# A one-core transformer layer: first columns of the modulation in another order with first features between them, and two groups of DVE work bound to a later point

## The chip, the cores and the metric

The kernel runs on one core of a Trainium2 chip. The metric is the device time of one execution in microseconds (us): median 2355.22 us of 3 runs, 2352.29 to 2355.99. The engines run their own instruction streams side by side: PE (TensorE, matrix products and transposes), DVE (VectorE), ACT (ScalarE), POOL (GpSimd), and SP (SyncE), which here issues most of the DMA transfers. Each engine takes its instructions in a fixed order; semaphores make it wait for what others produce.

## The reference, cut to what matters

One layer over 2048 latent tokens of width 1024, with 256 context tokens:

```
mod  = silu(c) @ w_ada + b_ada          # sh1 sc1 g1 sh2 sc2 g2, 1024 each
cmod = silu(c_ctx) @ w_ada + b_ada
hc = LN(ctx) * (1 + csc1) + csh1        # context: keys and values only
h  = LN(x) * (1 + sc1) + sh1
q, k, v, u, vg, ga, gb = split(h @ w_in)
y_attn = windowed attention (8 q heads, 2 kv heads, rope, sink, context keys)
y_gm   = gelu(u) * (ws @ LN(gelu(vg)) + bs)      # in chunks of 128 tokens
mix = (sigmoid(ga) * (y_attn @ w_pa) + sigmoid(gb) * (y_gm @ w_pb)) @ w_o
x  = LN(alpha * x + g1 * mix)
h2 = LN(x) * (1 + sc2) + sh2
x  = LN(alpha * x + g2 * moe(h2))       # 4 groups x 8 experts, top 2, SwiGLU
```

## The kernel before

Products are taken at 32 bits through two parts: every operand is split into a high part (a cast on ACT) and a low part (a subtraction on DVE, or on POOL in one place), and each product is three passes, high by high, low by high, high by low. `split` (L85) does this everywhere; `Wh` and `Wl` are the two parts of a piece of weights of 128x1024, loaded into one of three `raw` buffers by SP.

The work stands in four stages, whose limits in the trace are near 110, 560, 1470 and 2300 us.

**Start (`pass1`, before its loop over tokens).** `w_ada`'s columns for sh1 and sc1 come in four blocks of 512: blocks 0 and 1 are the shift, 2 and 3 the scale. Each block is four loads of 512 KB and 8 products (`ada_piece`, L265, 16 passes on PE). `ada_columns` (L270 to L275) copies a finished block on ACT, turns it into columns on PE, and DVE writes it into `modc`. Then come steps from the string `START`: `c0` to `c3` and `h0` to `h3` are `modulate` for the context tokens and for latent tokens 0 to 255, each for two of the eight 128-wide chunks of the width: PE transposes (L350), ACT applies scale and shift (L358, tile `hf`), the high part is taken on DVE (L364, `hTh`), the low part on DVE for the context and on POOL for latent tokens (L365, `hTl`), and for latent tokens SP writes `hf` to DRAM (`hT_d`, L367). Chunks 0 to 3 (`c0`, `c1`, `h0`, `h1`) need blocks 0 and 2; the others need 1 and 3. `x0`, `x1` and `a0`, `a1` are the k and v products for the two tiles of context and of latent tokens (L383, 24 products of 128x256 a tile); the second of the turns L394 that follow `a1` closes this stretch. `w4` to `w17` split weights. Instructions under `keep_in_program_order` keep their written order on their engine; the others are ordered by the scheduler's own simulation.

**Second pass (`pass2`)** goes over the latent tokens in four groups `g` of 512. For each, `spatial` multiplies the gated half by `wst` in eight parts (`gg`), each closed by a `scalar_tensor_tensor` on DVE (L840, in pairs), then `mixers` turns the result on PE (L850), splits it into `gh` and `gl`, and there are 8 steps `f` of gates and merge, with pieces `wf`. `between(g, f)` is called between these steps. In group 0 it appends `rows_ada` for f = 0 to 5: the other six blocks of `w_ada` for one row, as four 512 KB loads into `raw` and 8 multiply-adds on DVE (L760, L762). In groups 1 to 3 it calls `norms` for the four token tiles of the group before, for f = 0 to 3: the residual (L912), two layer norms (L94 to L100, L784, L785) and two writes. With `tc.issue_after(X)`, an instruction that is on X's engine is kept behind X; an instruction on another engine isn't bound by it. In the kernel before, `norms` is bound to `st["mixed"]`, the last split of the attention output, which is a DVE instruction.

**Experts (`moe`).** `prepare(s, j)` loads and splits pieces of the second expert's weights. `k.at[3]` is a PE instruction; the instructions of `prepare` run on ACT, DVE and SP.

The pieces that the change and the steps of the prediction touch are listed here.

Of the kernel before, what the change touches and what calls it, by code (L numbers as in the profile page):

```python
# [7 lines left out]
F32 = mybir.dt.float32  # L8
# [5 lines left out]
OP = mybir.AluOpType  # L14
# [4 lines left out]
P = 128  # L19
D = 1024  # L20
# [5 lines left out]
NQ = 8  # L26
# [107 lines left out]
            fn()  # L134


START = 'c0 c1 w5 c2 w6 w4 c3 x0 w7 h0 h1 h2 k w9 x1 h3 w8 a0 n0 a1 w10 t0 w11 t1 q0 q1 q2 q3 n1 q4 g0 q5 g1 l0 l1 w12 w14 w15 t2 l2 g2 s0 l3 g3 w17 l4 w16 s1 w13 l5'
PRM = dict(f0=0.2, f1=0.4, b1=0.4, b2=0.0, f2=0.8, f3=1.0, b3=1.2, pq=3, pk=5, mi=1, np=1, ps=16, pa=6)


# [8 lines left out]
def pass1(k):  # L149

    nc, tc, T = k.nc, k.tc, k.T
    with ExitStack() as ctx:
# [31 lines left out]
        def load_tile(t):  # L184
            load_x(t, T["x"][t * P:(t + 1) * P, :])
# [12 lines left out]
        def load_ada(i):  # L198
            if i < 16:
                ada[i] = wk.tile([P, 2, 512], F32, name="x", tag="x", bufs=4)  # L200
                pinned(nc.sync.dma_start(ada[i], T["ada1"][:, i // 4, 2 * (i % 4):2 * (i % 4) + 2, :]))

        for i in range(4):
            load_ada(i)
        cx = wk.tile([P, 2, D], F32, name="hTl", tag="hTl", bufs=2)
        for i in range(2):
            xin["c", i] = [cx[:, i, :]]
            pinned(nc.sync.dma_start(cx[:, i, :], T["ctx"][i * P:(i + 1) * P, :]))

        cols = ([(slice(2 * i, 2 * i + 2), slice(512, 768)) for i in range(4)]  # L210
                + [(slice(i, i + 1), slice(0, 512)) for i in range(8)]
# [23 lines left out]
        def norm_stats(key):  # L235
            x = xin[key]
            stats[key] = ln_stats(k, wk, x if len(x) == 2 else x[0], D, pin=key in range(2, PRM["ps"]))
# [16 lines left out]
            return x[h][:, kc * P:(kc + 1) * P]  # L254


        accs = {}

        def ada_piece(i):
            cb, kk = divmod(i, 4)  # L260
            if kk == 0:
                accs[cb] = ps.tile([2, 512], F32, name="pj", tag="pj", bufs=2)
            for j in range(2):
                kc = 2 * kk + j
                nc.tensor.matmul(accs[cb], k.sil[:, kc, :], ada[i][:, j, :], start=kc == 0, stop=kc == KC - 1)  # L265
            load_ada(i + 4)

        def ada_columns(cb):
            m2 = wk.tile([2, 512], F32, name="qr", tag="qr", bufs=1)
            nc.scalar.copy(m2, accs[cb])  # L270
            tp = ps.tile([P, 4, 2], F32, name="tr", tag="tr", bufs=1)
            for j in range(4):
                nc.tensor.transpose(tp[:, j, :], m2[:, j * P:(j + 1) * P], k.ident[0:2, 0:2])
            for s in range(2):
                nc.vector.scalar_tensor_tensor(k.modc[:, 2 * s + cb // 2, 4 * (cb % 2):4 * (cb % 2) + 4], tp[:, :, s],  # L275
                                               float(cb // 2), bcol[:, 4 * cb:4 * cb + 4], op0=OP.add, op1=OP.add)

        for i in range(16):
            ada_piece(i)
            if i in (2, 3):  # L280
                norm_stats(("c", i - 2))
            if i in (4, 5):
                norm_apply(("c", i - 4))
            if i in (4, 5):
                t = i - 4
                xin[t] = [wk.tile([P, 512], F32, name="x0", tag=("ph", "pl")[t], bufs=2) for _ in range(2)]
                for h in range(2):
                    pinned(nc.sync.dma_start(xin[t][h], T["x"][t * P:(t + 1) * P, h * 512:(h + 1) * 512]))
            if i in (8, 9):
                norm_stats(i - 8)  # L290
                norm_apply(i - 8)
            if 6 <= i < 10:
                load_w(i - 6)
            if 11 <= i < 15:
                wsplit(i - 11)
            if i > 4 and i % 4 == 1:
                ada_columns(i // 4 - 1)
        load_tile(2)
        load_tile(3)
        mk = wk.tile([P, 2, 2 * P], F32, name="hf", tag="hf", bufs=2)[:, 0, :]  # L300
        pinned(nc.sync.dma_start(mk, T["mask"]))
        sink = c.tile([P, NQ], F32, name="sink")
        pinned(nc.sync.dma_start(sink, bcast_row(T["sink"], NQ)))
        load_tab(0)
        load_tab(1)
        start[0] = False
# [398 lines left out]
def pass2(k):  # L705
    nc, tc, T = k.nc, k.tc, k.T
    k.late = k.ctx.enter_context(tc.tile_pool(name="late", bufs=1, reuse_waits="tile"))
    with ExitStack() as ctx:
# [120 lines left out]
        def spatial(g):  # L829

            uy, vv = st[g][1], st["vv"]
            if g == 0:
                tc.keep_in_program_order(nc.sync.dma_start(bst, T["bst"]))
            ws = wsplit(T["wst"].rearrange("p g q -> p (g q)"))
            for gg in range(8):
                tp = tr_bank()
                sp = tp[:, 0:256].rearrange("p (i d) -> p i d", d=HD)
                cs = slice(gg * HD, (gg + 1) * HD)
                mm3(sp, [x[:, gg * P:(gg + 1) * P] for x in ws], (vv[:, 0, :, cs], vv[:, 1, :, cs]), True, True)
                nc.vector.scalar_tensor_tensor(uy[:, 1, :, cs], sp, bst[:, gg:gg + 1], uy[:, 0, :, cs],  # L840
                                               op0=OP.add, op1=OP.mult)
# [318 lines left out]
        def between(g, f):  # L1160

            nonlocal g1, sh2, sc2, ln1g, ln1b, rws
            while due:
                due.pop(0)()
            if g == 0:
                if f < 6:
                    due.append(rows_ada(g1 if f < 2 else sh2 if f < 4 else sc2, f, 1.0 if f // 2 == 2 else 0.0))
                return
            t = 4 * (g - 1) + f
            if 1 <= f < 5:  # L1170
                turned[t - 1] = logit_rows(h2s[t - 1])
# [315 lines left out]
def moe(k):  # L1487
    nc, tc, T = k.nc, k.tc, k.T
    with ExitStack() as ctx:
# [213 lines left out]
        for i in range(NBL):  # L1703
            s, _, _, last = blocks[i]
            hidden(i)
            gate(i)
            with tc.issue_after(k.at[3]) if not i else nullcontext():
                rows(i + 1)
                if not i:
                    early_output(1)  # L1710
            if i:
                gather(i + GA)
                output(i - 1)
                evacuate(i - 1)
# [195 lines left out]
```

## Time and profile before

| | us |
|---|---|
| median of 3 runs | 2355.22 |
| profiled execution, own time | 2353.14 |
| its span, first to last instruction | 2351.1 |
| PE busy in the span | 2206.8 |
| DVE busy | 1749.7 |
| ACT busy | 1197.9 |
| POOL busy | 622.1 |

The profile is of one execution. It is read in this way: the busy times say which engine is nearest to the span, the table by windows says where that engine isn't busy, and the waits of an engine say what released it. A row `L383 <- POOL hTl L365: 2.6, 2, 1.5` says that the engine stood 2.6 us in all before line 383, twice, 1.5 us the longest, for what line 365 made on POOL.

### The profile page before, as it was taken

To read this page: it belongs to the slowest core of one execution; us is meant where nothing else is said; L and a number is where in the kernel's file an instruction comes from. 1 tells how busy PE (TensorE), PEld (TensorE's weight loads), DVE (VectorE), ACT (ScalarE), POOL (GpSimd) and SP (SyncE) were. 2 spreads that over 40 slices of the span, in tenths; PEclk is the share of its full clock that TensorE was granted. 3 is DMA by queue.
4 is the path that set the end of the run, shared out by engine and by line. 5 is a ranking of instruction groups with operands and counts; after the bars stand their busy time and mean duration, and the time that the engine had idled before them with its cause. 6 is when DMAs were issued, how large, how long until landed. Compare 5 with 4: busy or idle time off the path is not lost. (4 is left out here: it accounts for less than half of the span.)

```text
span 2351.1 us, 31795 instructions
## 1 busy us (share of the span) xinstructions
PE 2206.8 (94%) x11269; PEld 1813.8 (77%) x11269; DVE 1749.7 (74%) x3029; ACT 1197.9 (51%) x1673; POOL 622.1 (26%) x518
## 2 busy tenths in 40 slices
PE   7899999999999999999999999899999999999980
PEld 3789999997778788878887887587877777877760
DVE  4778888887675677577557858578898878696977
ACT  3566666655433333333424333356666666564755
POOL 1333333331000101011101113323353445243324
PEclk9899999999999999999999999899999999999995
DMA  8111111115674446544344434489998989797967
GB/s 313 64 59 59 55 59 42 41 42 170 197 239 153 152 144 185 161 151 150 112 156 153 153 117 188 152 271 322 338 339 290 330 280 331 234 360 235 337 215 295
DMA packets 126710, 449.34 MB, mean 191 GB/s; under 512 B 20763, under 2 KB 42195, under 8 KB 101973
## 3 DMA queue, kind: packets, MB, share of 16 engines
q1 hardware_dynamic: 113684, 405.29, 49.8%
q0 software_dynamic: 12864, 41.98, 7.5%
q8 instruction: 90, 1.47, 0.3%
q14 instruction: 72, 0.58, 0.1%
HBM read 382.66 MB, written 64.57 MB: 190 GB/s over the span
## 5 line engine op out<-in xcount | busy, mean ns | idle before, releaser
L85 DVE TENSOR_TENSOR mWl<-mraw,mWh 128x2048 fp32r<-128x2048 f32 x192 | 450.2, 2362 | 89.9 <-ACT mWh L85 89.0
L85 ACT CAST mWh<-mraw 128x2048 fp32r<-128x2048 f32 x192 | 363.7, 1909 | 176.0 <-PE h L1612 82.2
L100 POOL TENSOR_TENSOR mv<-mv,mhalf 128x1 f32<-128x1 f32 x58 | 56.7, 981 | 664.2 <-DVE mv L99 657.9
L1612 PE MATMUL h<-mWh,xh 128*128 128x512 f32 x784 | 218.2, 400 | 12.4 <-ACT xh L85 7.9
L85 DVE TENSOR_TENSOR Wl<-raw,Wh 128x1024 fp32r<-128x1024 f32 x140 | 170.4, 1220 | 77.5 <-ACT Wh L85 76.8
L85 ACT CAST Wh<-raw 128x1024 fp32r<-128x1024 f32 x140 | 146.1, 1047 | 139.0 <-PE mm L743 66.2
L1612 PE MATMUL h<-mWl,xh 128*128 128x512 f32 x784 | 214.7, 394 | 0.0
L742 PE MATMUL mm<-hh,Wl 128*128 128x512 f32 x512 | 201.1, 393 | 5.5 <-DVE Wl L85 5.5
L741 PE MATMUL mm<-hh,Wh 128*128 128x512 f32 x512 | 202.7, 396 | 2.3 <-ACT Wh L85 1.6
L743 PE MATMUL mm<-hl,Wh 128*128 128x512 f32 x512 | 200.8, 392 | 0.0
L1660 POOL DMA_INDIRECT acc_d<-yo,lst x48 | 144.1, 3003 | 153.6 <-DVE yo L1654 95.7
L1612 PEld LDWEIGHTS h<-mWh,xh 128*128 128x128 f32 x784 | 145.3, 189 | 46.5 <-ACT xh L85 9.8
L1612 PEld LDWEIGHTS h<-mWl,xh 128*128 128x128 f32 x784 | 146.8, 188 | 32.9
L383 PE MATMUL pj<-wq,hTh 128*128 128x256 f32 (+1 forms) x544 | 151.9, 355 | 1.6 <-DVE hTh L364 1.4
L1577 POOL DMA_INDIRECT xg<-h_d,lst x48 | 79.9, 1665 | 206.6 <-PE tr L1598 98.7
L85 ACT CAST ph<-pt 128x512 fp32r<-128x512 f32 x184 | 93.4, 520 | 73.4 <-PE pt L572 69.9
L1612 PE MATMUL h<-mWh,xl 128*128 128x512 f32 x464 | 127.0, 394 | 0.0
L548 ACT ACTIVATE Sb<-Sb,mx 128x641 f32<-128x641 f32 (+1 forms) x128 | 105.4, 824 | 40.3 <-DVE mx L543 31.3
L541 DVE CUSTOM_DVE_ANT_0 Sb<-S,mask,sink 128x640 f32<-128x640 f32 (+1 forms) x128 | 110.2, 861 | 18.9 <-PE S L537 15.8
L85 DVE TENSOR_TENSOR pl<-pt,ph 128x512 fp32r<-128x512 f32 x184 | 109.0, 604 | 19.2 <-ACT ph L85 17.4
L1612 PE MATMUL y<-mWh,gh 128*128 128x512 f32 x392 | 112.2, 406 | 8.1 <-ACT mWh L85 3.3
L742 PEld LDWEIGHTS mm<-hh,Wl 128*128 128x128 f32 x512 | 96.7, 189 | 26.4 <-DVE Wl L85 7.1
(385 smaller groups left out, 5371.9 us busy)
## 6 DMA issues: line engine op xcount, KB each, us to landing
mraw<-mw SPq DMA_DIRECT2D x192, 1024.0 KB, 7.3
raw<-wf SPq DMA_DIRECT2D x96, 512.0 KB, 3.7
raw<-ada SPq DMA_DIRECT2D x32, 512.0 KB, 4.8
raw<-wo SPq DMA_DIRECT2D x32, 512.0 KB, 4.2
x<-x SPq DMA_DIRECT2D x30, 512.0 KB, 4.3
x<-ada SPq DMA_DIRECT2D x16, 512.0 KB, 5.4
hT_d<-hf SPq DMA_DIRECT2D x32, 256.0 KB, 2.2
raw<-hT_d SPq DMA_DIRECT2D x16, 512.0 KB, 4.9
```

The lines of the kernel that those rows point to most:

```text
L85: return k.nc.scalar.copy(hi, src), (eng or k.nc.vector).tensor_sub(lo, src, hi)
L100: nc.gpsimd.tensor_tensor(mv[:, 3:4], mv[:, 2:3], k.mhalf, op=OP.pow)
L383: ins = nc.tensor.matmul(box[0][:, :n], x[:, kc, ts], wpart(y, kc, slice(c0, c0 + n))[:, 0, :], start=q == 0, stop=q == 3 * KC - 1)
L541: nc.vector.tensor_tensor_reduce(x[:, :nk], S[:, :nk], mask[:, mi, :nk], 1.0, sink[:, h:h + 1], OP.add, OP.max, mx[:, s:s + 1])
L548: nc.scalar.activation(Sb[s][:, :nk + 1], Sb[s][:, :nk + 1], AF.Exp, bias=mx[:, 2 + s:3 + s], scale=1.0, accum_out=mx[:, 4 + s:5 + s])
L741: nc.tensor.matmul(out, lh, rh, start=first, stop=False)
L742: nc.tensor.matmul(out, ll, rh, start=False, stop=False)
L743: nc.tensor.matmul(out, lh, rl, start=False, stop=last)
L1577: ins = nc.gpsimd.indirect_dma_start(out=xg[i][0:n, :], out_offset=None, in_=k.h2_d[:, :], in_offset=bass.IndirectOffsetOnAxis(ap=place(i) ...
L1612: ins = nc.tensor.matmul(accs[m], a[:, ks], b[:, c0:c0 + 512], start=first and i + j == 0, stop=last and j == 1 and i == len(t) - 1)
L1660: nc.gpsimd.indirect_dma_start(out=k.acc_d[:, :], out_offset=bass.IndirectOffsetOnAxis(ap=l[:, 0:1], axis=0), in_=yo[0:n, :], in_offset=No ...
```

## The change

There are five edits. (A) The blocks of `w_ada` are loaded and used in the order 0, 2, 1, 3; the steps c0, c1 run behind piece 10, and h0, h1 behind piece 12 of the 16, inside the loop over the pieces, and are taken out of `START`. The context tokens are loaded as four tiles of 128x512 rather than two of 128x1024. The mask goes through another buffer. The function definitions that the steps need are moved ahead of the loop unchanged, which shifts their lines: L350 becomes L322, L383 becomes L355. (B) `rows_ada` is called for f = 1 to 6 and bound to `st["sp"]`, the last L840 instruction so far. (C) `norms` for f above 0 is bound to the same. (D) In the experts, two calls of `prepare` are bound to `k.at[3]`. The fifth edit stores `st["sp"]`.

```diff
-START = 'c0 c1 w5 c2 w6 w4 c3 x0 w7 h0 h1 h2 k w9 x1 h3 w8 a0 n0 a1 ...
+START = 'w5 c2 w6 w4 c3 x0 w7 h2 k w9 x1 h3 w8 a0 n0 a1 ...
...
-                pinned(nc.sync.dma_start(ada[i], T["ada1"][:, i // 4, 2 * (i % 4):2 * (i % 4) + 2, :]))
+                pinned(nc.sync.dma_start(ada[i], T["ada1"][:, (0, 2, 1, 3)[i // 4], 2 * (i % 4):2 * (i % 4) + 2, :]))
...
-        cx = wk.tile([P, 2, D], F32, name="hTl", tag="hTl", bufs=2)
         for i in range(2):
-            xin["c", i] = [cx[:, i, :]]
-            pinned(nc.sync.dma_start(cx[:, i, :], T["ctx"][i * P:(i + 1) * P, :]))
+            xin["c", i] = [wk.tile([P, 512], F32, name="cx", tag=n, bufs=2 if i else 1) for n in (("oT", "oT") if i else ("t1", "t2"))]
+            for h in range(2):
+                pinned(nc.sync.dma_start(xin["c", i][h], T["ctx"][i * P:(i + 1) * P, h * 512:(h + 1) * 512]))
...
             if i > 4 and i % 4 == 1:
                 ada_columns(i // 4 - 1)
+            for n in {10: ("c0", "c1"), 12: ("h0", "h1")}.get(i, ()):
+                steps[n]()
...
-                nc.vector.scalar_tensor_tensor(uy[:, 1, :, cs], sp, bst[:, gg:gg + 1], uy[:, 0, :, cs],
-                                               op0=OP.add, op1=OP.mult)
+                st["sp"] = nc.vector.scalar_tensor_tensor(uy[:, 1, :, cs], sp, bst[:, gg:gg + 1], uy[:, 0, :, cs],
+                                                          op0=OP.add, op1=OP.mult).ins
...
-                if f < 6:
-                    due.append(rows_ada(g1 if f < 2 else sh2 if f < 4 else sc2, f, 1.0 if f // 2 == 2 else 0.0))
+                if 1 <= f < 7:
+                    with tc.issue_after(st["sp"]):
+                        due.append(rows_ada(g1 if f < 3 else sh2 if f < 5 else sc2, f - 1, 1.0 if f > 4 else 0.0))
...
-                with tc.issue_after(st["mixed"]):
+                with tc.issue_after(st["sp" if f else "mixed"]):
                     h2s[t] = norms(t, rr[f])
...
             if i == 1:
-                prepare(1, 0)
-                prepare(1, 1)
+                with tc.issue_after(k.at[3]):
+                    prepare(1, 0)
+                    prepare(1, 1)
```

How the instructions then stand on PE at the start, first before. L265 are the passes over blocks of `w_ada`, L273 the turns of a finished block, L350 the transposes of context tokens (`hTl` is the buffer that held them), and L383 the k and v products.

```order
L273 MATMUL tr<-ident,qr 128x2 x4
L265 MATMUL pj<-x,sil 2x512 x6
L273 MATMUL tr<-ident,qr 128x2 x4
L265 MATMUL pj<-x,sil 2x512 x6
L273 MATMUL tr<-ident,qr 128x2 x4
L265 MATMUL pj<-x,sil 2x512 x6
L350 MATMUL pt<-ident,hTl 128x128 x4
L273 MATMUL tr<-ident,qr 128x2 x4
L350 MATMUL pt<-ident,hTl 128x128 x4
L383 MATMUL pj<-wq_114,hTh 128x256
L383 MATMUL pj<-wq_114,hTl 128x256
L383 MATMUL pj<-wq_115,hTh 128x256
```

And on PE after the change, in two pieces of the same stretch: `x_192` and `x_202` are latent tokens, `cx` is the context, and the last rows shown are the last passes of the loop.

```order
L322 MATMUL pt<-ident,x_192 128x128
L322 MATMUL pt<-ident,x_202 128x128
L274 MATMUL tr<-ident,qr 128x2 x4
L322 MATMUL pt<-ident,cx 128x128 x4
L265 MATMUL pj<-x,sil 2x512 x2
L322 MATMUL pt<-ident,cx 128x128 x4
L355 MATMUL pj<-wq_114,hTh 128x256
L355 MATMUL pj<-wq_114,hTl 128x256
L355 MATMUL pj<-wq_115,hTh 128x256
```

```order
L355 MATMUL pj<-wq_116,hTh 128x256
L355 MATMUL pj<-wq_116,hTl 128x256
L355 MATMUL pj<-wq_119,hTh 128x256
L265 MATMUL pj<-x,sil 2x512 x4
L274 MATMUL tr<-ident,qr 128x2 x4
```

Eight transposes of latent tokens, eight more of the context and twelve k and v products now stand ahead of the last four passes of the loop; all of them stood behind the loop before.

On DVE in group 0 of the second pass, before: L760 and L762 are `rows_ada` (`aacc`), L840 closes the parts of `spatial`, `Wl` is the low part of a piece of weights.

```order
L760 TENSOR_SCALAR aacc<-raw,sil 128x512
L85 TENSOR_TENSOR Wl<-raw,Wh 128x1024
L762 SCALAR_TENSOR_TENSOR aacc<-raw,sil,aacc 128x512 x2
L94 BN_STATS st<-vg 128x6
L762 SCALAR_TENSOR_TENSOR aacc<-raw,sil,aacc 128x512
L98 BN_AGGR mv<-st 128x2
L840 SCALAR_TENSOR_TENSOR yh<-tr,bst,yh 128x4x64
L762 SCALAR_TENSOR_TENSOR aacc<-raw,sil,aacc 128x512
L99 TENSOR_SCALAR mv<-mv 128x1
L840 SCALAR_TENSOR_TENSOR yh<-tr,bst,yh 128x4x64
L762 SCALAR_TENSOR_TENSOR aacc<-raw,sil,aacc 128x512 x3
L85 TENSOR_TENSOR Wl<-raw,Wh 128x1024
```

The same place after the change, where L843 is the former L840 and L763, L765 are `rows_ada`:

```order
L843 SCALAR_TENSOR_TENSOR yh<-tr,bst,yh 128x4x64 x2
L85 TENSOR_TENSOR Wl<-raw,Wh 128x1024
L843 SCALAR_TENSOR_TENSOR yh<-tr,bst,yh 128x4x64 x2
L85 TENSOR_TENSOR Wl<-raw,Wh 128x1024
L843 SCALAR_TENSOR_TENSOR yh<-tr,bst,yh 128x4x64 x2
L85 TENSOR_TENSOR Wl<-raw,Wh 128x1024
L890 TENSOR_TENSOR sg<-sg,mm 128x512
L843 SCALAR_TENSOR_TENSOR yh<-tr,bst,yh 128x4x64 x2
L763 TENSOR_SCALAR aacc<-raw,sil 128x512
L765 SCALAR_TENSOR_TENSOR aacc<-raw,sil,aacc 128x512
```

All of `rows_ada` now stands behind the fourth pair of the closings.

On DVE in group 1, before, from the last `Wl` but two ahead of the first pair of L840: `rr` and `x` are rows in `norms`, of two tiles.

```order
L85 TENSOR_TENSOR Wl<-raw,Wh 128x1024
L98 BN_AGGR mv<-st 128x2 x2
L99 TENSOR_SCALAR mv<-mv 128x1
L784 SCALAR_TENSOR_TENSOR x<-rr,mv,sc_7747 128x1024
L99 TENSOR_SCALAR mv<-mv 128x1
L784 SCALAR_TENSOR_TENSOR rr<-rr,mv,ln1g 128x1024
L785 SCALAR_TENSOR_TENSOR x<-x,mv,sh_7489 128x1024
L785 SCALAR_TENSOR_TENSOR rr<-rr,mv,ln1b 128x1024
L85 TENSOR_TENSOR Wl<-raw,Wh 128x1024
L94 BN_STATS st<-rr 128x6 x2
L840 SCALAR_TENSOR_TENSOR yh<-tr,bst,yh 128x4x64 x2
```

After the change:

```order
L787 SCALAR_TENSOR_TENSOR x<-rr,mv,sc_7729 128x1024
L85 TENSOR_TENSOR Wl<-raw,Wh 128x1024
L788 SCALAR_TENSOR_TENSOR x<-x,mv,sh_7475 128x1024
L85 TENSOR_TENSOR Wl<-raw,Wh 128x1024
L843 SCALAR_TENSOR_TENSOR yh<-tr,bst,yh 128x4x64 x2
L85 TENSOR_TENSOR Wl<-raw,Wh 128x1024
L843 SCALAR_TENSOR_TENSOR yh<-tr,bst,yh 128x4x64 x2
L85 TENSOR_TENSOR Wl<-raw,Wh 128x1024
L843 SCALAR_TENSOR_TENSOR yh<-tr,bst,yh 128x4x64 x2
L85 TENSOR_TENSOR Wl<-raw,Wh 128x1024
L890 TENSOR_TENSOR sg<-sg,mm 128x512
L843 SCALAR_TENSOR_TENSOR yh<-tr,bst,yh 128x4x64 x2
```

The norms of the second tile are gone from between the weights' low parts; they follow behind the last pair. On PE and ACT the order in the experts is the same in both kernels.

## Rows read from the trace of the kernel before

**Rows 1.** The page's busy times: engine, us (share of the span), instructions.

```profile
PE 2206.8 (94%) x11269; PEld 1813.8 (77%) x11269; DVE 1749.7 (74%) x3029; ACT 1197.9 (51%) x1673; POOL 622.1 (26%) x518
```

**Rows 2.** Windows: length, busy us of PE, PEld, DVE, ACT, POOL, clock, DMA, GB/s.

```profile
0.00:110.00 110.00, 88.84 (x416) 55.30 (x417) 61.59 (x147) 49.83 (x93) 30.19 (x43) 0.94 0.57 198
```

**Rows 3.** Groups of PE's instructions, 0 to 40 us: busy, mean | idle before.

```profile
L265 PE MATMUL pj<-x,sil 128*2 128x512 f32 x64 | 30.5, 622 | 7.4 <-DMA x<-ada 7.3
```

**Rows 4.** Windows within the start, columns as in group 2.

```profile
20.00:40.00 20.00, 19.41 (x58) 4.38 (x57) 7.87 (x22) 7.37 (x12) 1.09 (x2) 1.00 1.01 376
...
60.00:64.00 4.00, 4.00 (x20) 4.00 (x20) 2.24 (x7) 0.27 (x1) 1.28 (x2) 0.50 0.00 0
```

**Rows 5.** PE's waits, 40 to 66 us: total us, times, longest.

```profile
PE pj L383 <- POOL hTl L365: 2.6, 2, 1.5
PE pj L383 <- DVE hTh L364: 1.4, 1, 1.4
PE pj L383 <- DVE hTl L365: 0.8, 1, 0.8
PE pt L350 <- ACT hf L358: 0.8, 2, 0.5
```

**Rows 6.** PE's timeline, 39 to 66 us: start, us, instruction [idle before].

```profile
38.47 1.45 PE L265 MATMUL pj<-x,sil 128*2 128x512 f32 x3
39.85 0.66 PE L350 MATMUL pt<-ident,hTl 128*128 128x128 f32 x4
...
45.48 0.38 PE L383 MATMUL pj<-wq,hTl 128*128 128x256 f32 x1 [0.76 <-DVE hTl L365]
...
47.51 0.28 PE L383 MATMUL pj<-wq,hTl 128*128 128x256 f32 x1
...
47.86 0.28 PE L383 MATMUL pj<-wq,hTl 128*128 128x256 f32 x1
...
65.32 0.38 PE L394 MATMUL tr<-ident,kd 128*128 128x128 f32 x2
```

**Rows 7.** ACT's timeline at the start.

```profile
42.80 1.02 ACT L358 ACTIVATE hf<-pt,modc 128x256 f32<-128x256 f32 x2 [0.79 <-DVE hTl L365]
```

**Rows 8.** PE's waits in group 0, 600 to 680 us.

```profile
PE tr L850 <- DVE yh L840: 2.6, 1, 2.6
PE mm L741 <- ACT Wh L85: 2.1, 2, 1.6
PE mm L742 <- DVE Wl L85: 1.0, 2, 0.8
```

**Rows 9.** Windows in group 0, columns as in group 2.

```profile
611.00:616.00 5.00, 4.96 (x15) 3.93 (x16) 2.60 (x5) 1.04 (x1) 0.00 (x0) 0.66 0.91 315
...
626.00:631.00 5.00, 5.00 (x21) 4.02 (x20) 3.20 (x4) 2.12 (x3) 0.00 (x0) 0.78 0.78 242
```

**Rows 10.** ACT's timeline in group 0, 604 to 613 us.

```profile
608.68 1.04 ACT L85 CAST Wh<-raw 128x1024 fp32r<-128x1024 f32 x1 [3.06 <-DMA raw<-wf]
```

**Rows 11.** DVE's timeline in group 0, 596 to 632 us.

```profile
621.32 0.75 DVE L762 SCALAR_TENSOR_TENSOR aacc<-raw,sil,aacc 128x512 f32<-128x512 f32 x1 [1.34 <-DMA raw<-ada]
```

**Rows 12.** PE's waits in group 1, 780 to 850 us.

```profile
PE mm L742 <- DVE Wl L85: 1.5, 1, 1.5
...
PE mm L743 <- DVE mv L99: 0.9, 1, 0.9
PE tr L850 <- DVE yh L840: 0.5, 1, 0.5
```

**Rows 13.** DVE's timeline in group 1, 780 to 856 us.

```profile
802.56 0.74 DVE L784 SCALAR_TENSOR_TENSOR vg<-vg,mv,sg 128x512 f32<-128x512 f32 x1
803.22 1.28 DVE L94 BATCH_NORM_STATS2 st<-rr 128x6 f32<-128x512 f32 x2
...
820.52 1.22 DVE L85 TENSOR_TENSOR Wl<-raw,Wh 128x1024 fp32r<-128x1024 f32 x1
...
846.05 1.29 DVE L85 TENSOR_TENSOR gl<-tr,gh 128x512 fp32r<-128x512 f32 x2 [4.86 <-ACT gh L85]
```

More of the change, by code (lines that the diff above doesn't have):

```diff
@@ L134, in emit @@
             fn()
-START = 'c0 c1 w5 c2 w6 w4 c3 x0 w7 h0 h1 h2 k w9 x1 h3 w8 a0 n0 a1 w10 t0 w11 t1 q0 q1 q2 q3 n1 q4 g0 q5 g1 l0 l1 w12 w14 w15 t2 l2 g2 s0 l3 g3 w17 l4 w16 s1 w13 l5'
+START = 'w5 c2 w6 w4 c3 x0 w7 h2 k w9 x1 h3 w8 a0 n0 a1 w10 t0 w11 t1 q0 q1 q2 q3 n1 q4 g0 q5 g1 l0 l1 w12 w14 w15 t2 l2 g2 s0 l3 g3 w17 l4 w16 s1 w13 l5'
 PRM = dict(f0=0.2, f1=0.4, b1=0.4, b2=0.0, f2=0.8, f3=1.0, b3=1.2, pq=3, pk=5, mi=1, np=1, ps=16, pa=6)
@@ L254, in chunk @@
             return x[h][:, kc * P:(kc + 1) * P]
-        accs = {}
+        accs, cbs = {}, (0, 2, 1, 3)
         def ada_piece(i):
-            cb, kk = divmod(i, 4)
+            cb, kk = cbs[i // 4], i % 4
             if kk == 0:
@@ L266, in ada_piece, with ada_columns @@
             load_ada(i + 4)
-        def ada_columns(cb):
+        def ada_columns(i):
+            cb = cbs[i]
             m2 = wk.tile([2, 512], F32, name="qr", tag="qr", bufs=1)
@@ L276, in ada_columns @@
                                                float(cb // 2), bcol[:, 4 * cb:4 * cb + 4], op0=OP.add, op1=OP.add)
[L278 to L306, printed above, removed]
         mask = c.tile([P, 2, 640], BF16, name="mask")
@@ L650, in pass1 @@
         steps["f"] = flush
+        for i in range(16):
+            ada_piece(i)
+            if i in (2, 3):
+                norm_stats(("c", i - 2))
+            if i in (4, 5):
+                norm_apply(("c", i - 4))
+            if i in (4, 5):
+                t = i - 4
+                xin[t] = [wk.tile([P, 512], F32, name="x0", tag=("ph", "pl")[t], bufs=2) for _ in range(2)]
+                for h in range(2):
+                    pinned(nc.sync.dma_start(xin[t][h], T["x"][t * P:(t + 1) * P, h * 512:(h + 1) * 512]))
+            if i in (8, 9):
+                norm_stats(i - 8)
+                norm_apply(i - 8)
+            if 6 <= i < 10:
+                load_w(i - 6)
+            if 11 <= i < 15:
+                wsplit(i - 11)
+            if i > 4 and i % 4 == 1:
+                ada_columns(i // 4 - 1)
+            for n in {10: ("c0", "c1"), 12: ("h0", "h1")}.get(i, ()):
+                steps[n]()
+        load_tile(2)
+        load_tile(3)
+        mk = wk.tile([P, 2, P], F32, name="kd", tag="kd").rearrange("p a b -> p (a b)")[:, 0:2 * P]
+        pinned(nc.sync.dma_start(mk, T["mask"]))
+        sink = c.tile([P, NQ], F32, name="sink")
+        pinned(nc.sync.dma_start(sink, bcast_row(T["sink"], NQ)))
+        load_tab(0)
+        load_tab(1)
+        start[0] = False
         ada_columns(3)
```

## The prediction, made before the changed kernel ran

> **What bounds the kernel now.** I read the busy times first, then the windows by stage, then PE's waits in the stretches that the change touches, and last the timelines around these waits. PE is busy 2206.8 of 2351.1 us [rows 1], so 144.3 us are left in which it does nothing, and an edit shortens the kernel if it takes PE's idle time, or PE's time at the low clock, or nothing. The start is the richest place: in the first 110 us PE is busy 88.84 [rows 2], so 21.2 us are idle. There the loop over `w_ada` is fed by DMA: 7.4 us of idle before its passes, nearly all <-DMA [rows 3], and the DMA engines are full from 20 to 40 us (share 1.01, [rows 4]). Behind it PE waits 2.6 + 1.4 + 0.8 + 0.8 = 5.6 us for the first features [rows 5], and from 60 to 64 us it is busy all the time, but at a granted clock of 0.50, which is 1.2 GHz [rows 4]. The last turn before the q products starts at 65.32 [rows 6]: that is the time to shorten. In group 0 of the second pass PE waits 5.7 us [rows 8] and has a clock of 0.66 and 0.78 in two windows of 5 us behind these waits [rows 9]. In groups 1 to 3 a wait of 1.5 us for a low part `Wl` comes once a group [rows 12]; the same two main rows came in each of the three groups.
>
> **A, the start.** No arithmetic is added or taken away on PE; four context loads stand for two of the same bytes. What moves: 16 transposes and 12 products now stand ahead of the loop's last passes. Four transposes take 0.66 us [rows 6], so 16 take 2.6; the three passes of one product advance 47.86 - 47.51 = 0.35 us, so 12 take 1.4; 4.0 us in all. The loop can hide part of it. Its end slips by nothing if the last piece's arrival sets it (the DMA share of 1.01 speaks for that), and at most by 4.0 less the free time in the loop. That free time, with 64 passes at (39.85 - 38.47)/3 = 0.46 us, is 39.85 - 7.4 - 29.4 = 3.0 us, of which other transposes in the loop take about 2 (twelve at 0.66 for four): so the slip lies between 0 and 3. I take 1.4, the middle, and the loop ends at 41.25.
>
> What is late next is c2, which needs the last block. Before, the first product on its low part stands at 45.48, 5.63 us behind the loop's end [rows 6], and on the way c2's activation waited 0.79 us for DVE's low part of c1 [rows 7], and shared ACT and DVE with c0 and c1, which are gone from there. I take off the 0.79 and some 1.2 us for that other work, which leaves 3.65 us, so 44.9. Of the four tiles' 96 products 84 are left: 84 x 0.117 = 9.8 us; with 8 transposes of h2 and h3 (1.3) PE would be through at 56.0. I leave 2 us for waits and low clock that stay: 58 in place of 65.32, a gain of **7.3 us**. The ends: if the slip is 3, waits of 4 us stay and the clock loss stays, the end is 63.8, a gain of 1.5; if the loop doesn't slip and nothing is lost, 54.3, a gain of 11.
>
> The clock is where I could be wrong. The rows show that PE was busy throughout 60 to 64 us at half speed behind waits of up to 1.5 us each [rows 4, 5]; a full-speed 4 us would have done twice the work, so 2.0 us were lost there. After the change, these waits go (h0 and h1 have their POOL subtractions done during the loop), but a new one of up to 3.6 us stands between the loop's end and c2's products, which twelve products of the second context tile may half fill. The Trainium skill, "TensorE: Matmul & The Clock Gate", section "HAM oscillation — how this bites in real kernels", tells that where bursts of matmul are shorter than the waits between them, the clock falls again each time and the next burst starts cold. That speaks against part of A: by that rule the new wait would bring back the low clock that the old waits had brought. The trace agrees for the old waits, with the 0.50 from 60 to 64 us. It is the first rival below, priced from rows.
>
> On SP two writes of `hf` now stand between loads; each is 256 KB, together some 1.4 us at the 376 GB/s of [rows 4]. What they delay is weights of the q products, which are used behind 65 us; I cost it at nothing, up to 1.4 us if they are late.
>
> **B, the rows of group 0.** `rows_ada` now stands behind the last pair of L840. So no `ada` piece holds a `raw` buffer while `wf` pieces are wanted: ACT's cast waited 3.06 us for such a piece [rows 10], which is the wait of 1.6 for `Wh` on PE; and L762 waited 1.34 us for its own piece [rows 11] in front of the L840 that PE waited 2.6 us for [rows 8]. These waits should go, with the low clock behind them: 4.96 x 0.34 = 1.7 and 5.00 x 0.22 = 1.1 us [rows 9]. The most is 5.7 + 2.8 = 8.5. Against it: two smaller waits of 0.5 and 0.2 us (the rest of [rows 8]) stand later and stay, 0.7; PE's wait for yh in the other groups, where no `rows_ada` is in the way, is still 0.5 [rows 12]; and 0.8 I leave for the loads of `ada`, which now come while gates use `raw`. That is 8.5 - 0.7 - 0.5 - 0.8 = **6.5 us**; ends 0 (the same loads collide later) and 8.5. The DVE work itself, 8 operations of 0.75 us a block, is spread over steps in which PE has its weights.
>
> **C, the norms of groups 1 to 3.** A tile's norms are seven operations of about 1.28 us [rows 13], 9.0 us, that leave the space ahead of the `Wl` at 820.52, for which PE waited 1.5 us. That wait goes: 3 x 1.5 = 4.5. But the order also sets one statistics instruction (0.64) and one L784 (0.74) ahead of an earlier `Wl`, for which PE waits already 0.9 us: it comes about 1.35 us later, 3 x 1.35 = 4.0. The sum is +**0.5 us**, with ends +4.5 (the earlier wait doesn't grow) and -4.0 (the later one doesn't go). Behind the last pair the norms stand among the `gl` splits, where DVE idles 4.86 us at a stretch [rows 13].
>
> **D, the experts.** `k.at[3]` is on PE and `prepare` issues nothing there, so the binding makes no edge; the order on PE and ACT is unchanged. 0.
>
> **Sum.** 7.3 + 6.5 + 0.5 = 14.3 us of gain. The profiled execution took 2353.14, so 2338.8; it lay 2.1 below the median of 2355.22, so by the median **2341 us**. The forecast's own range is 2336 to 2346.
>
> **The rivals.**
> 1. *The start keeps its waits and its low clock.* The wait for c2 takes the place of the old ones, and the burst behind it runs at 1.2 GHz. For it speaks [rows 4]: this place has given half clock after waits of one to two us. Against it: less work is left behind the wait. A gives about 1.2 in place of 7.3: 2355.2 - 8.2 = 2347.
> 2. *Group 0's waits move.* The six blocks are now read within fewer steps through the same three buffers, and `wf` pieces wait behind them at f = 2 to 7 as they did before. For it: 24 pieces, four a block, of 512 KB have to pass in any case. Against it: the gates behind the last pair want their pieces one by one, with a product of 24 passes between two of them. B gives 1.5: 2355.2 - 9.3 = 2346.
> 3. *No measurable change.* Both of these at once, with C at its lower end: 1.2 + 1.5 - 2 = 0.7: about 2354.
> 4. *Slower: the moved norms land on PE.* In groups 1 to 3, the second tile's 9.0 us push the `gl` splits back, on which the merge's products wait; PE has nothing else there. If all of it lands, 27 us are lost against 13.8 from A and B: 2368. It decides from 4.6 us a group (13.8/3). For it: the norms do stand between the `gl` splits. Against it: DVE has 4.86 us free just there, and the other work of gate products on PE goes on without DVE.
>
> **How the numbers follow.** A comparison of this kernel can tell about 0.2%, 4.7 us, from no change: faster is under 2350.5, slower above 2359.9. Chances: the forecast 0.50, rival 1 0.18, rival 2 0.13, rival 3 0.12, rival 4 0.07. So faster 0.50 + 0.18 + 0.13 = 0.81, same 0.12, slower 0.07. The range: from 2332 (A and B near their upper ends: 2355.2 - 11 - 8.5 - 4.5 = 2331) to 2354, which takes in rivals 1 and 2 and half of rival 3; left out are half of rival 3 (0.06), rival 4 (0.07) and some 0.05 below.
>
> **What would show it.** In the changed kernel's trace: (A) the last L265 pass ends between 40 and 43 us, the second turn of L394's successor starts near 58 and not behind 63, and there is no 4 us window at 0.50; (B) no wait for yh of over 1 us in group 0, none for `Wh` near 610, and clock 1.00 from 606 to 631; (C) the 1.5 us wait for `Wl` gone in each group, the wait at the earlier `Wl` near 2.2 us; (D) the experts' stage as long as before, within 1 us. The prediction is wrong if the start ends behind 62 us, if group 0 shows new waits of 4 us in sum for `raw`, or if PE waits for `gl` or for rows of `norms` in groups 1 to 3.

## The result and the profile after

The changed kernel took 2340.01 us (median of 5 runs, 2335.03 to 2340.39) against 2355.22 (5 runs, 2352.27 to 2359.17): ratio 0.9929, 95% interval 0.9911 to 0.9946. The forecast was 2341 us, with a range of 2332 to 2354. Its profiled execution took 2335.28 us, with a span of 2333.4. Two executions far outside the others are left out of every figure, one of the kernel before (11304 us) and one of B alone (4261 us); the second is the profiled one of its kernel, so B alone has no trace that can be compared.

The busy line of its page, for [rows 1]:

```profile
PE 2200.9 (94%) x11269; PEld 1807.9 (77%) x11269; DVE 1748.0 (75%) x3029; ACT 1195.2 (51%) x1673; POOL 637.2 (27%) x518
```

The span fell by 17.7 us, PE's busy time by only 5.9: two thirds of the gain were idle time of PE. Where it came can be read by matching DVE's instructions of the two traces, kind by kind and in order, and taking the median shift of those that started in a stretch of the kernel before (negative: earlier in the changed one). The gain of a stage is the step from one column to the next:

| place (us in before) | 100 | 530 | 760 | 980 | 1180 | 1420 | 2310 |
|---|---|---|---|---|---|---|---|
| changed kernel | -6.9 | -6.2 | -12.9 | -14.3 | -15.3 | -16.7 | -17.8 |
| forecast | -7.3 | -7.3 | -13.8 | -14.0 | -14.1 | -14.3 | -14.3 |

By this one pair of traces the start gave 6.9 (forecast 7.3), group 0 6.7 (6.5), groups 1 to 3 3.8 (0.5), and the experts 1.1 (0). Of the 6.9, 0.7 are lost again by 530 us. The runs below show that the first figure is not what the edit is worth.

**The start.** PE's timeline of the changed kernel around the end of the loop and the turns (L366, before: L394), as in [rows 6]:

```profile
39.56 3.59 PE L265 MATMUL pj<-x,sil 128*2 128x512 f32 x8
43.88 0.40 PE L274 MATMUL tr<-ident,qr 2*128 2x2 f32 x4 [0.72 <-ACT qr L271]
45.71 0.66 PE L322 MATMUL pt<-ident,x 128*128 128x128 f32 x4 [1.43 <-ACT hf L330]
...
46.33 0.28 PE L355 MATMUL pj<-wq,hTl 128*128 128x256 f32 x1
...
58.17 0.38 PE L366 MATMUL tr<-ident,kd 128*128 128x128 f32 x2
61.03 0.66 PE L366 MATMUL tr<-ident,kd 128*128 128x128 f32 x2 [2.48 <-DVE kr L370]
```

The turn at 65.32 came at 58.17, for which 58 was forecast. The way there was another: the loop ended at 43.15 (39.56 + 3.59), 3.3 us later than before and not 1.4; then the first product on c2's low part came at 46.33, 3.18 us behind it and not 3.65, and from there to the turn PE had one wait of 0.8. The waits from 36 to 66 us, for [rows 5]:

```profile
PE tr L366 <- DVE kr L370: 2.5, 1, 2.5
PE pt L322 <- ACT hf L330: 1.4, 1, 1.4
PE pj L355 <- DVE vC L376: 0.8, 1, 0.8
PE tr L274 <- ACT qr L271: 0.7, 1, 0.7
```

None of the old four is left but the one for `hf`, which grew. The windows around the turns, columns as in [rows 2], for [rows 4]:

```profile
56.00:60.00 4.00, 2.55 (x22) 2.31 (x20) 3.40 (x12) 1.57 (x4) 1.78 (x3) 1.00 0.00 0
60.00:64.00 4.00, 2.97 (x8) 2.47 (x9) 3.31 (x7) 1.51 (x2) 0.84 (x3) 0.62 0.02 4
```

From 52 to 60 us, while the products run, the clock is 1.00; it falls behind the turn at 58.17, where PE waits 2.48 us for `kr`: 0.62 from 60 to 64 us.

**Group 0.** PE's waits from 600 to 680 us, for [rows 8], and two windows for [rows 9]:

```profile
PE mm L745 <- DVE Wl L85: 0.8, 1, 0.8
PE tr L853 <- DVE yh L843: 0.5, 1, 0.5
```

```profile
612.00:617.00 5.00, 4.30 (x24) 3.38 (x23) 4.93 (x10) 1.07 (x2) 0.00 (x0) 1.00 0.59 169
617.00:622.00 5.00, 5.00 (x27) 3.98 (x25) 2.91 (x4) 1.04 (x2) 0.00 (x0) 1.00 0.77 238
```

5.7 us of waits are 1.3, with one more of 0.2 for `gh`, and the clock stays at 1.00, which is 2.4 GHz, from 606 to 631 us.

**Groups 1 to 3.** PE's waits in group 1, 768 to 838 us, for [rows 12], and DVE's timeline there, for [rows 13]:

```profile
PE mm L744 <- DVE rr L909: 1.3, 1, 1.3
PE mm L746 <- DVE Wl L85: 1.1, 1, 1.1
PE tr L853 <- DVE yh L843: 0.5, 1, 0.5
```

```profile
784.91 1.29 DVE L94 BATCH_NORM_STATS2 st<-vg 128x6 f32<-128x512 f32 x2 [5.13 <-ACT vg L828]
...
787.05 0.69 DVE L94 BATCH_NORM_STATS2 st<-rr 128x6 f32<-128x512 f32 x1
787.65 0.14 DVE L99 TENSOR_SCALAR mv<-mv 128x1 f32<-128x1 f32 x1
787.71 0.74 DVE L787 SCALAR_TENSOR_TENSOR vg<-vg,mv,sg 128x512 f32<-128x512 f32 x1
788.37 1.22 DVE L85 TENSOR_TENSOR Wl<-raw,Wh 128x1024 fp32r<-128x1024 f32 x1
```

In the kernel before the first of these instructions stands at 799.23:

```profile
799.23 1.29 DVE L94 BATCH_NORM_STATS2 st<-vg 128x6 f32<-128x512 f32 x2 [5.32 <-ACT vg L825]
```

The wait of 1.3 for `rr` is not one of the norms: L909 closes the output products of the group before, and the kernel before waits 1.4 us for the same line (L906). The wait of 1.5 for the late `Wl` is gone. The statistics and the L787 stand in front of the earlier `Wl` as the order showed, but that wait grew only from 0.9 to 1.1 here, and to 1.5 and 1.8 in groups 2 and 3.

### The profile page after: what moved, and what is told of

Its sections match the earlier page's. It is cut to its first block, busy times and chain, and to the rows that moved or that the text cites. A ratio compares the mean times of both kernels' runs of the same rounds, so it can differ in the third digit from the quotient of the medians.

```text
span 2333.4 us, 31796 instructions
## 1 busy us (share of the span) xinstructions
PE 2200.9 (94%) x11269; PEld 1807.9 (77%) x11269; DVE 1748.0 (75%) x3029; ACT 1195.2 (51%) x1673; POOL 637.2 (27%) x518
## 5 line engine op out<-in xcount | busy, mean ns | idle before, releaser
L100 POOL TENSOR_TENSOR mv<-mv,mhalf 128x1 f32<-128x1 f32 x58 | 68.2, 1178 | 641.4 <-DVE mv L99 607.3
L1616 PE MATMUL h<-mWh,xh 128*128 128x512 f32 x784 | 218.9, 401 | 10.8 <-ACT xh L85 8.6
L355 PE MATMUL pj<-wq,hTh 128*128 128x256 f32 (+1 forms) x544 | 149.5, 351 | 0.8 <-DVE vC L376 0.8
L1581 POOL DMA_INDIRECT xg<-h_d,lst x48 | 86.0, 1792 | 211.2 <-PE tr L1602 103.9
```

What stands on the lines that cost most here:

```text
L100: nc.gpsimd.tensor_tensor(mv[:, 3:4], mv[:, 2:3], k.mhalf, op=OP.pow)
L355: ins = nc.tensor.matmul(box[0][:, :n], x[:, kc, ts], wpart(y, kc, slice(c0, c0 + n))[:, 0, :], start=q == 0, stop=q == 3 * KC - 1)
L1581: ins = nc.gpsimd.indirect_dma_start(out=xg[i][0:n, :], out_offset=None, in_=k.h2_d[:, :], in_offset=bass.IndirectOffsetOnAxis(ap=place(i) ...
L1616: ins = nc.tensor.matmul(accs[m], a[:, ks], b[:, c0:c0 + 512], start=first and i + j == 0, stop=last and j == 1 and i == len(t) - 1)
```

## The experiments

All were timed against the kernel before, run on the same chip beside them; a ratio of 0.001 is 2.4 us. The kernel before itself spread over 11 to 13 us in each of these sets (31 runs in the first, 2347.70 to 2360.14), so single differences under 2 us aren't told apart. The parts are named A (start), B (group 0), C (groups 1 to 3), D (experts). The offsets in the text are those of the table above, in each kernel's own trace, against the same trace of before.

**A alone.** The changed kernel without B, C and D:

```diff
-                if 1 <= f < 7:
-                    with tc.issue_after(st["sp"]):
-                        due.append(rows_ada(g1 if f < 3 else sh2 if f < 5 else sc2, f - 1, ...))
+                if f < 6:
+                    due.append(rows_ada(g1 if f < 2 else sh2 if f < 4 else sc2, f, ...))
...
-                with tc.issue_after(st["sp" if f else "mixed"]):
+                with tc.issue_after(st["mixed"]):
...
-                with tc.issue_after(k.at[3]):
-                    prepare(1, 0)
-                    prepare(1, 1)
+                prepare(1, 0)
+                prepare(1, 1)
```

> The start's edit alone. Theory (the three edits act each in its own stretch, and their gains add): 6 to 7 us faster, all of it before 70 us; the first a1 turn near 58 us, and the offset against the kernel before stays between -6.9 and -6.2 us from 100 us up to the second pass and on through it. Rival (the edits help one another: A only shifts what follows, and part of what looks like B's and C's gain comes with the shift): the offset grows beyond -6.9 in group 0 or in groups 1 to 3, to -8 or more, without their edits.

Measured: ratio 0.9995 (0.9983 to 1.0006), so 1.2 us faster, and no difference within the interval. Its trace is 5.0 ahead at 100 us, 4.4 at 530, and only 2.7 at 760: group 0 gave 1.7 back. Group 1 took 2.6 more, and the experts 5.2; this profiled execution took 2358.56 us, the slowest of the 11 (median 2351.11), so its losses can't be put down to the edit. PE's wait there, 600 to 680 us:

```profile
PE tr L853 <- DVE yh L843: 6.9, 1, 6.9
```

and what stood in front of that closing on DVE:

```profile
617.70 2.32 DVE L765 SCALAR_TENSOR_TENSOR aacc<-raw,sil,aacc 128x512 f32<-128x512 f32 x3 [3.83 <-DMA raw<-ada]
```

So the theory that 6 to 7 us would stay fell, and the rival (A mends the later places) has nothing for it: this trace lost there.

**B alone.** The kernel before with the two edits of B (`st["sp"]` and the call of `rows_ada`).

> The edit of group 0 alone. Theory: 6 to 7 us faster, gained between 600 and 630 us; PE's waits in 600 to 680 us fall from 5.7 to under 2 us and the clock is 1.00 from 606 to 631. Rival (the clock there depends on where the waits fall, and it was A's shift that mended it): only the waits go, 4 us, and windows with a clock of under 0.9 stay.

Measured: ratio 0.9963 (0.9947 to 0.9979), 8.7 us faster (5 to 12.5). B is the largest part. What it does to the waits and to the clock is read in the kernel without A, below.

**C alone.** The kernel before with `st["sp"]` and the one line of `norms`.

> The edit of groups 1 to 3 alone. Theory from the trace of the changed kernel: 3 to 4 us faster, 1.0 to 1.4 in each of the three groups; the wait of 1.5 us for Wl near the closings goes, and the earlier one for Wl grows from 0.7 to 0.9 us to 1.1 to 1.8. Rival (the prediction as written): the two cancel, 0.5 us faster, since the earlier wait grows by 1.35 us each time.

Measured: ratio 0.9991 (0.9979 to 1.0002), 2.1 us faster, not clear of no change. Its trace goes from -2.9 at 760 to -8.8 at 1420, a gain of 5.9 in the three groups, and then loses 5.4 in the experts. PE's waits in group 1, 780 to 850 us, show the exchange of [rows 12] by itself:

```profile
PE mm L743 <- DVE Wl L85: 1.1, 1, 1.1
PE mm L741 <- DVE rr L906: 0.6, 1, 0.6
PE tr L850 <- DVE yh L840: 0.5, 1, 0.5
```

0.9 became 1.1, and the 1.5 is gone.

**D alone.** The kernel before with `prepare(1, 0)` and `prepare(1, 1)` under `issue_after(k.at[3])`.

> The edit of the experts alone. Theory: no edge is made, so 0, within 1 us in the experts' stage of the trace; what differs between executions is not the edit's. Rival: the one register load that moves on SP changes when expert weights are fetched, and the 1.1 us that the changed kernel gained behind 1470 us comes with it.

Measured: ratio 1.0005 (0.9990 to 1.0020): 0, as forecast, to within the 3.5 us of the interval. The order on every engine is that of the kernel before, so this trace is also a second look at that program. It loses 2.2 us in the experts, more than the 1 us of the theory; executions of one program differ by more than that there (below), so neither that bound nor the rival's 1.1 us can be told. It is 2.5 us ahead at 100 us, and its wait in group 0 is not 2.6 but

```profile
PE tr L850 <- DVE yh L840: 4.0, 1, 4.0
```

**The changed kernel again, and without A.** The kernel without A has the changed kernel's B, C and D with the start of before. Both were run twice, in two sets.

> The changed kernel once more, beside the parts on the same chip. Theory 1 (parts add, with sizes as the separate runs had them: start 1.7, group 0 9.9, groups 1 to 3 3.0 us): 14 to 16 us faster than the kernel before, and a second profile again shows the wait for yh in group 0 below 1 us. Theory 2 (the start's 7 us are whole where group 0's rows are bound, and given back where they aren't): the same total, so this run serves as the other half of the next one.

> The changed kernel with the start as before (edits of group 0, groups 1 to 3 and the experts alone). Theory 1 (the start is worth 1.7 us wherever it stands): 12 to 14 us faster than before, 2 us behind the changed kernel. Theory 2 (the start's gain is whole when group 0 no longer waits for its rows' loads, since then nothing gives it back): 8 to 9 us faster than before, 5 to 7 us behind the changed kernel. In the trace of either the first a1 turn lies at 62 to 66 us.

> The changed kernel a third time, on the same chip as the next three. Theory (the start's edit gains 3 to 4 us by 100 us, where the profile of before had lost 2.5 to 3 more to the clock than other executions do, and 1 to 3 of them are left at the end): 1 to 3 us faster than the kernel with the start as before. Rival (the start's gain is given back wholly): equal to it within 1 us. Its profile at 100 us: 5 to 7 us ahead of the first profile of before.

> The changed kernel with the start as before, a second time. Theory: 1 to 3 us slower than the changed kernel of the same job, and at 100 us again 2 to 3 us ahead of the first profile of before, although the start's program is the same: the low clock there differs between executions. Rival: equal to the changed kernel, and the place at 100 us within 1 us of the first profile.

| | ratio | interval | at 100 | 530 | 760 | 1420 | 2310 |
|---|---|---|---|---|---|---|---|
| changed, again | 0.9938 | 0.9920 to 0.9956 | -5.4 | -4.9 | -12.9 | -16.7 | -18.3 |
| without A | 0.9938 | 0.9920 to 0.9956 | -3.1 | -3.0 | -10.3 | -15.6 | -19.3 |
| changed, third time | 0.9917 | 0.9899 to 0.9936 | -6.0 | -5.3 | -12.9 | -16.0 | -12.8 |
| without A, second time | 0.9932 | 0.9914 to 0.9950 | -0.5 | -0.3 | -7.4 | -11.9 | -16.9 |

With A and without it the kernel is as fast in the first set, and 3.5 us apart (0.0015 of 2355) in the second, less than either interval; by the medians the one with A is 1.8 and 0.7 us faster. The theory that the start's gain is whole once B is in (5 to 7 us) fell; 0 to 4 us is what is left. The columns show why A looked larger. Six executions of the old start (before, C alone, D alone, B shifted, twice without A) stand at 0, -2.8, -2.5, -1.8, -3.1 and -0.5 at 100 us, mean -1.8; five of the new one (the changed kernel three times, A alone, and the kernel with all norms bound) at -6.9, -5.4, -6.0, -5.0 and -7.1, mean -6.1. The edit gives 4.3 us there and 3.7 at 530, and the execution that the prediction was worked out from was the slowest of the six. The second execution without A was expected 2 to 3 us ahead at 100 us and is 0.5 ahead. The clock makes the difference between executions of one start. The windows of 60 to 64 and 68 to 72 us in the first and the second execution without A:

```profile
60.00:64.00 4.00, 4.00 (x27) 3.88 (x26) 2.24 (x7) 0.33 (x2) 1.28 (x2) 0.74 0.00 0
68.00:72.00 4.00, 4.00 (x21) 3.21 (x20) 1.25 (x5) 1.25 (x1) 0.56 (x1) 1.00 0.00 0
```

```profile
60.00:64.00 4.00, 4.00 (x21) 4.00 (x20) 2.24 (x7) 0.27 (x1) 1.28 (x2) 0.50 0.00 0
68.00:72.00 4.00, 4.00 (x13) 3.09 (x12) 2.14 (x6) 0.99 (x2) 0.67 (x2) 0.57 0.02 4
```

One program, the same waits in front of it to 0.3 us, 27 products or 21 in the first 4 us, 21 or 13 in the second: one execution is 3.1 ahead, the other, at 0.50 and 0.57 like the trace of before, 0.5. What the clock takes in these 8 us is 1.0 in the first (4 x 0.26) and 3.7 in the second (4 x 0.50 + 4 x 0.43); the 2.7 between them is about the 2.6 by which they stand apart. PE's waits in group 0 without A, in the first execution, are close to those of the changed kernel:

```profile
PE mm L742 <- DVE Wl L85: 1.3, 2, 0.8
PE tr L850 <- DVE yh L840: 0.5, 1, 0.5
```

Group 0 gives 7.3 and 7.0 us there without A, and the clock is 1.00 in every 5 us from 606 to 631 in both executions, so the rival of B alone (that A's shift mended the clock) fell. Over all traces group 0 gives 5.9 to 8.1 us in the eight with B, and between -1.7 and 1.5 in those of A, C and D alone and of B shifted.

**B's calls shifted, but not bound.**

```diff
-                if f < 6:
-                    due.append(rows_ada(g1 if f < 2 else sh2 if f < 4 else sc2, f, ...))
+                if 1 <= f < 7:
+                    due.append(rows_ada(g1 if f < 3 else sh2 if f < 5 else sc2, f - 1, ...))
```

> Group 0 alone, with the calls of rows_ada moved from f = 0 to 5 to f = 1 to 6 but not bound to the last closing: on DVE the first pair of closings is then free of rows, and eight multiply-adds still stand among the other three pairs. Theory (rows of a late load in front of a closing make PE wait for yh; the bond is what helps): a wait for yh of 1 us or more stays in 600 to 680 us, the gain is under 5 us. Rival (only the loads' place on SP matters, and the later call gives that): the wait for yh is 0.5, and the gain is that of the full edit, 9 to 10 us.

Measured: ratio 1.0007 (0.9995 to 1.0018), no gain at all. PE's waits, 600 to 680 us, and the two windows behind:

```profile
PE tr L850 <- DVE yh L840: 4.3, 1, 4.3
PE tr L741 <- DVE yh L840: 1.7, 2, 1.5
```

```profile
621.00:626.00 5.00, 1.97 (x8) 1.57 (x8) 4.16 (x7) 1.51 (x3) 0.00 (x0) 0.68 0.76 233
626.00:631.00 5.00, 4.93 (x14) 3.94 (x15) 2.59 (x4) 1.02 (x3) 0.00 (x0) 0.63 0.69 208
```

The later call is not enough: the wait for `yh` is still 4.3 us. The bond makes the difference, and what it does is that no multiply-add which waits for a load stands in front of a closing on DVE.

**All norms bound.**

```diff
-                with tc.issue_after(st["sp" if f else "mixed"]):
+                with tc.issue_after(st["sp"]):
```

> The changed kernel with the norms of the first token tile bound to the last closing as well, in groups 1 to 3, so that no norm stands among the head's low parts. Theory (the waits of 1.1, 1.5 and 1.8 us for Wl that are left there come from one statistics instruction and one L787 in front of it, and DVE has room behind the closings): these waits fall to under 0.5 us, 2 to 4 us faster than the changed kernel. Rival (the norms of two tiles at once, 18 us of DVE, then land on PE's wait for gl or on the turns of the logits): new waits of over 2 us a group, not faster or slower by up to 10 us.

Measured: ratio 0.9967 (0.9955 to 0.9979), against 0.9938 for the changed kernel in the same set: 7 us of the 15 are lost. The first half of the theory held, no wait for `Wl` is left near the closings. But from 760 to 980 it falls from -12.7 to -8.1, where the changed kernel gains 1.4 and 1.8 in its first two executions and nothing in the third. PE's timeline, 915 to 940 us, then SP's and DVE's in front of it:

```profile
931.27 0.79 PE L744 MATMUL mm<-hh,Wh 128*128 128x512 f32 x1 [3.83 <-ACT Wh L85]
933.01 0.80 PE L745 MATMUL mm<-hh,Wl 128*128 128x512 f32 x1 [0.94 <-DVE Wl L85]
```

```profile
919.31 0.80 SPq L827 DMA_DIRECT2D vg<-vg_d  x2
926.64 3.38 SPq L732 DMA_DIRECT2D raw<-wf  x2
```

```profile
925.26 0.69 DVE L94 BATCH_NORM_STATS2 st<-vg 128x6 f32<-128x512 f32 x1 [2.68 <-ACT vg L828]
925.87 0.73 DVE L765 SCALAR_TENSOR_TENSOR aacc<-raw,sil,aacc 128x512 f32<-128x512 f32 x1
```

In the changed kernel's second execution `vg`'s load goes out at 915.23, and the next `wf` piece at 922.44:

```profile
922.44 6.57 SPq L732 DMA_DIRECT2D raw<-wf  x3
```

The clock behind the wait, 930 to 935 us, is 0.62:

```profile
930.00:935.00 5.00, 2.79 (x6) 1.90 (x7) 4.59 (x8) 3.11 (x4) 0.86 (x2) 0.62 0.53 127
```

In group 1, too, blocks of `rows_ada` are read one at a time, through the same `raw` buffers. The `wf` piece goes out when the multiply-add at 925.87 (921.68 in the changed kernel) has freed a buffer. In front of that stands a statistic of `vg`, for which DVE idles 2.68 us, and `vg`'s load goes out behind the last token tile's logits on PE, which start at 917.44 (913.35). So the norms bound later put the logits later, these the load of `vg`, this the multiply-add, and the piece comes so late that PE waits 4.8 us. I read this chain from the order and the times; it was not tried by itself. In this trace 4.6 us go in group 1, and 3.5 more in the experts.

**Only the context inside the loop.** The changed kernel with `{10: ("c0", "c1")}` in the loop, and `h0 h1` in front of `h2` in `START`.

> The changed kernel with only c0 and c1 inside the loop, and h0, h1 back behind it (column order 0, 2, 1, 3 kept). Theory (the loop's end slips because PE has 16 transposes and 12 products more in front of it, not because the data come late): the last pass ends 1 to 2 us earlier than the 43.1 of the changed kernel, but h0's and h1's low parts on POOL, 1.3 us each, come in front of h2's again, and the wait on POOL's hTl is back; the first a1 turn is at 58 to 61, the total within 2 us of the changed kernel. Rival (the loop's end is set by the DMA engines): the last pass ends at 43 as well.

Measured: ratio 0.9940 (0.9924 to 0.9957), against 0.9917 in the same set: 5 us slower than the changed kernel, where 2 at most were expected. Its last passes and its turn:

```profile
38.30 3.60 PE L265 MATMUL pj<-x,sil 128*2 128x512 f32 x8
...
61.45 0.38 PE L366 MATMUL tr<-ident,kd 128*128 128x128 f32 x2
```

The loop ends at 41.9, 1.2 to 2.7 earlier than in the changed kernel's three executions. In the first of these PE shows no wait from 31.85 us to the loop's end at 43.15. So PE's work in front of the last passes sets the loop's end, not the DMA engines, which the rival said. The turn comes 1.8 to 3.3 later. Not the wait for POOL's `hTl` came back in front of it, as I had expected; these waits are new or longer (that for `vC` was 0.8):

```profile
PE tr L366 <- DVE kd L399: 1.6, 1, 1.6
PE pj L355 <- DVE vC L376: 1.4, 1, 1.4
```

**The turns ahead of the weight splits.** `... a1 t0 t1 w10 w11 q0 ...` for `... a1 w10 t0 w11 t1 q0 ...` in `START`.

> The changed kernel with the k turns t0 and t1 ahead of the weight splits w10 and w11 in START, so that the subtraction for kr (0.41 us) no longer stands behind a weight's low part on DVE. Theory: the wait of 2.5 us for kr between the two turns falls to about 1.5, and the q products start 1 us earlier, so up to 1 us faster, below what the comparison can tell. Rival: w10 comes later by as much, the q products wait for its low part instead, and nothing is gained by 110 us.

Measured: ratio 0.9928 (0.9911 to 0.9944), the same as the changed kernel's 0.9917 within the intervals. The wait for `kr` went, and another came in its place on the same turn, with one for an activation behind it:

```profile
PE pt L322 <- ACT x L242: 1.9, 1, 1.9
PE tr L366 <- DVE mv L102: 1.7, 1, 1.7
```

At 100 us it is at -4.3, behind all three of the changed kernel. The rival is nearer. None of these versions beats the changed kernel.

## Why the prediction was right, point by point, and where it wasn't

The time came within 1 us of the forecast, in part by luck: A was taken too large, C and, by the times, B too small, and the errors cancelled. That most of the gain comes from waits of PE, and which waits go, was right.

- *A, 7.3 us:* the term was mis-sized. Two steps failed. "I take 1.4, the middle" of 0 to 3 for the slip: it is 3.3 in the first trace and 3.1 to 4.8 in the others with A's loop, above the upper end each time, since A's work in front of the loop's last passes isn't hidden. And the old start's 65.32 was called "the time to shorten": it is the latest of six executions (the others 63.7 to 65.0), and time won at the turn doesn't all last. The new turn comes at 58.0 to 59.6, near the 58 forecast, because only one wait was left and c2's chain was 0.5 shorter than taken. That is 5.8 us earlier as a mean; behind it stand the wait for `kr` and a low clock, and 4.3 are left at 100 us, 3.7 at 530. By total times it is 0 to 4. Rival 1 (2347) had A's size, about 1.2, but its mechanism didn't come: PE waits for c2 (0.7 and 1.4 us), and the clock behind is 1.00; the slow stretch comes behind `kr`.
- *The clock:* the prediction priced 2.0 us from one execution. Executions of one program differ by more than that at 100 us. The Trainium skill, "TensorE: Matmul & The Clock Gate", section "What's actually happening", says that the watching of activity runs free, doesn't begin with the kernel, and that the same kernel so has more or fewer slow products at its start from run to run. The traces here show such a difference in the middle of work: 0.50 or 0.74 in the same 4 us of one program, above.
- *B, 6.5 us:* right in mechanism and size by the traces (6.7; 7.3 and 7.0 without A), and 8.7 (5 to 12.5) by times. The row of 2.6 us for yh [rows 8] was a small case of a wait that is 4.0 in the next execution and 6.9 in A's. Rival 2 fell for group 0. What it describes, weights behind `ada` pieces in `raw`, came up in group 1 of the kernel with all norms bound.
- *C, 0.5 us:* the term was mis-sized. "It comes about 1.35 us later, 3 x 1.35": on DVE that is so, the `Wl` begins 3.46 us behind the statistics in front of it and not 2.13. But the wait, 0.9, 0.7 and 0.8 before, grew by 0.2, 0.8 and 1.0, 2.0 in all rather than 4.0. In group 1 the statistics began 14.3 us earlier than before (784.91 for 799.23), while the wait ended 13.0 earlier (789.64 for 802.63): DVE had a lead on PE that the prediction didn't count. With 4.5 for the wait that went this is 2.5; the traces show 3.8, and 5.9 for C alone. The trace of before is also the best of the four without C in these groups: the other three lose 0.4 to 3.1 there. By total times C alone is 2.1 and not clear of 0. Rival 4 fell: PE shows no wait for `gl` or for rows of norms.
- *D, 0:* right as far as total times can tell, 3.5 us.
- *The signs:* those of B all came. Three of the others missed: the loop ended at 43.15 and not by 43, the earlier `Wl` waits 1.1 to 1.8 and not 2.2, and the experts' stage is 1.1 shorter in the first trace and up to 5 off in others.
- *The sum:* the four parts alone give 1.2 + 8.7 + 2.1 - 1.2 = 10.8 us, all together 14.6 to 19.5. The intervals are wide enough for the difference, but B and C together without A (14.6 and 16.0) also give more than their two parts. In the traces the experts' stage takes 1 to 5 us off in five of the seven executions with B and C in the form of the change (and adds 3.2 and 1.3 in two), and adds 1 to 5 in the four kernels without B. Much of that is between executions: the changed kernel's own three stand at -1.1, -1.6 and +3.2. Some kernels also have a few instructions of that stage in another order. What does it I haven't found; it stays open.

## What to carry to other kernels

An operation that waits for a load should not stand on an in-order engine in front of one that PE waits for: moving its call was worth nothing, binding it behind was worth 7 us in the traces. Before a wait or a low clock in a trace is priced, look at the same place in a second execution of the same program; here the start differed by 3 us and a wait in group 0 by 1.4 to 1.8 between executions. And work that is bound to a later point takes its buffers along: binding one more tile's norms, 9 us of DVE in each group, lost 7 us, of which 4.6 in the trace lie where a load that nothing in the edit names went out later.

## What the runs showed of the hardware that I had not expected

The spread of the kernel before goes with its granted clock: in the first set its 7 runs at a mean clock of 0.978 or 0.979 took 2349.4 us on average, its 10 at 0.973 to 0.975 took 2356.9. And one wait is not always followed by the same clock, even in one program. At the start of the second pass of the changed kernel PE waits 2.56 us, in the first execution and in the second:

```profile
557.62 0.50 PE L744 MATMUL mm<-Wh,hh 128*128 128x512 f32 x1 [2.56 <-ACT Wh L85]
```

```profile
558.95 0.79 PE L744 MATMUL mm<-Wh,hh 128*128 128x512 f32 x1 [2.56 <-ACT Wh L85]
```

The windows behind keep 1.00 in the first and show 0.51 in the second:

```profile
560.00:565.00 5.00, 4.50 (x20) 3.38 (x19) 2.28 (x2) 1.08 (x2) 0.00 (x0) 1.00 0.83 240
```

```profile
560.00:565.00 5.00, 5.00 (x13) 3.92 (x12) 2.14 (x6) 2.06 (x2) 0.00 (x0) 0.51 0.81 255
```
